# First layer: the values of all heads projected ahead of the attention, with tokens on the partitions, by way of DRAM

## The chip, the cores and the metric

One core of a Trainium2 chip runs the whole program as one launch. The metric is the device time of that launch in microseconds (us), median of several executions. TensorE (PE, with its weight loads PEld), VectorE (DVE), ScalarE (ACT) and GpSimd (POOL) each run their own instructions in order and wait for each other by semaphores; all transfers are issued from SyncE (SP) in one in-order queue.

## What is computed

A model of four layers on 1024 tokens of width 1024. Only the first matters here: RMS norm, one projection into queries, keys and values for three attention groups (dilations 1, 4 and 16) of 16 heads with 64 columns, softmax attention in each, a mix of the three by their log-sum-exps, a gate, and an output projection.

```python
def dilated_attention_mixer(h, w_in, w_out, rel_bias):
    B, S, _ = h.shape
    proj = h @ w_in
    n_qkv = 3 * N_GROUPS_A * ATTN_WIDTH
    qkv = proj[..., :n_qkv].reshape(B, S, 3, N_GROUPS_A, ATTN_HEADS, HEAD_DIM)
    z = proj[..., n_qkv:]
    outs, lses = [], []
    for g, (window, dilation) in enumerate(DILATED_GROUPS):
        o, l = dilated_group_attention(qkv[:, :, 0, g], qkv[:, :, 1, g], qkv[:, :, 2, g],
                                       rel_bias, window, dilation)
        outs.append(o)
        lses.append(l)
    wts = jax.nn.softmax(jnp.stack(lses), axis=0)
    o = jnp.sum(wts[..., None] * jnp.stack(outs).astype(jnp.float32), axis=0)
    o = o.reshape(B, S, ATTN_WIDTH).astype(h.dtype)
    return (o * jax.nn.silu(z)) @ w_out
```

The second layer is a state-space mixer whose tables (powers and kernels from a_re, a_im, log_dt, b, c) don't depend on the tokens. The third and fourth are scaled and shifted by "modulations", products of one vector with w_mod_2, which don't depend on the tokens either. Both are prepared during the first layer.

## The kernel before, in words

All large products are made in three parts: an operand is split into a high part in a format that TensorE takes at full rate (fp32r) and a rest, and high x high, high x rest and rest x high are summed (`mm3`, line 158; its matmuls are all line 168). A tile of 512 columns over a depth of 1024 is 24 matmuls. ScalarE rounds a weight chunk (`w_split`, line 154: wh), VectorE takes the rest (line 155: wl). `stream` (line 1023) keeps four chunks of 512 KB on their way and one split ahead.

`attn` (line 240) first loads the eight tiles of x, normalizes them (`prenorm`) and turns them into aTh and aTl, the normalized input with features on the partitions, split (`to_aT`, lines 215 to 221). The projections start among that: `stream` is opened after the fourth tile.

Then it goes over 8 head pairs p and, within each, 3 groups g. `project(p, g)` (line 312) makes queries, keys and values, each a column of 128 features by 1024 tokens in two halves (`proj_cm`): 6 halves of 24 matmuls. For g below 2 the queries and keys are split by ScalarE and VectorE out of the accumulator (lines 351 and 353) and GpSimd copies the key's parts (line 357). The values are copied by ScalarE into a tile `v` in the order of the dilation (line 343). `steps` (line 377) makes a list of functions: two `vtr`, each of which transposes four 128x128 pieces of `v` on TensorE (line 385) and copies them to V by VectorE (line 386), then ten functions with scores S (lines 399 to 404), the masked row minimum (VectorE, line 412), exponentials (ScalarE, line 414), transposes of them (line 425) and the product with V (lines 132 and 135).

These functions are put on a background list `self.bg`. Every eighth matmul of a projection is a tick, and `tick` takes as many functions from the list as `pace` has set, so that the steps of one group run among the projections of the next. On the same list come `finish` of a head pair (five functions, lines 460 to 538: the statistics turned and passed through DRAM, the weights of the three groups, the weighing and the sum, mostly on VectorE), `ssm_setup` (line 611: five functions, then for each of eight blocks `ca` on GpSimd, `kmat`, and `wj` on VectorE and TensorE, all of which use the one buffer u_A in turn) and the 24 modulations (`mod_jobs`, line 1124: a load of 512 KB, 16 multiply-adds on VectorE of line 1153's form in two functions, and a sum over partitions by ScalarE, GpSimd and TensorE, lines 1159 to 1164). Setup runs in the first eight groups, four functions each; the modulations after it, two per group at first, then one. The tile framework orders each engine's instructions when the program is built, by its own estimate of what is ready.

Of the kernel before, what the change touches and what calls it, by code (L numbers as in the profile page):

```python
# [11 lines left out]
F32 = mybir.dt.float32  # L12
F32R = mybir.dt.float32r
AF = mybir.ActivationFunctionType
# [61 lines left out]
class Ker:  # L76
# [163 lines left out]
    def attn(self, zs):  # L240

        nc, tc, A = self.nc, self.tc, self.A
        w = A["attn_w_in"][0]
# [8 lines left out]
        with ExitStack() as es:  # L252
            qp = es.enter_context(tc.tile_pool(name="qp", bufs=2, reuse_waits="tile"))
            ap = es.enter_context(tc.tile_pool(name="ap", bufs=2, reuse_waits="tile"))
            with ExitStack() as xs:
                p = xs.enter_context(tc.tile_pool(name="l0in", bufs=1, side="right", reuse_waits="tile"))
                g = self.bcast(p, A["attn_pre_norm"][0], "gpre")
                for i in range(8):
                    x = p.tile([128, 1024], F32, tag="x", name=self.uid("x"), bufs=2)
                    nc.sync.dma_start(x, A["x"][0, i * 128:(i + 1) * 128, :])  # L260
                    self.to_aT(self.prenorm(p, x, g), i)
                    if i == 3:
                        weights = self.stream([(w, c) for c in cols])
                self.attn_tables(p)
            side = es.enter_context(ExitStack())
            sp = side.enter_context(tc.tile_pool(name="su", bufs=1, side="right", reuse_waits="tile"))
            setup = deque(self.ssm_setup(sp))
# [43 lines left out]

            def project(p, g):
                T = {}
# [4 lines left out]
                for what in range(3):  # L318
# [4 lines left out]
                    if what == 2:  # L323
                        T[2] = tile_("v", F32, 1)
                    elif split:
# [9 lines left out]
                    for hf in range(2):  # L335
                        ps = self.proj_cm(h, l, hf * 512, parts=1 if p or g or what else 2)
# [5 lines left out]
                        if what == 2 or not split:  # L342
                            nc.scalar.activation(at(T[what], g, hf), pv, AF.Copy, scale=sc)
                            continue
# [32 lines left out]
            def steps(p, g, T, bt, st, O):  # L377
                V = ap.tile([128, 8, 128], F32, tag="V", name=self.uid("V"), bufs=1)
                vT = T[2]

                def vtr(hf):
                    t = self.pt()
                    for k in range(4):
                        c = (hf * 4 + k) * 128
                        nc.tensor.transpose(t[:, k * 128:(k + 1) * 128], vT[:, c:c + 128], self.ident)
                    nc.vector.tensor_copy(V[:, hf * 4:hf * 4 + 4, :], t.rearrange("p (k n) -> p k n", n=128))

# [60 lines left out]
                out = [lambda: vtr(0), lambda: vtr(1)]  # L448
# [91 lines left out]
            fin, mods = None, None  # L540
            for p in range(8):
# [3 lines left out]
                for g in range(3):  # L545
                    self.pace(18)
# [3 lines left out]
                    if g == 0 and fin:  # L550
                        todo.insert(1, fin[0])
                        todo.insert(5, fin[1])
                        todo.insert(9, fin[2])
                        todo.insert(12, fin[3])
                        todo.append(fin[4])
                    if setup:
                        for k in range(min(4, len(setup))):
                            todo.insert(2 + 4 * k, setup.popleft())
                        if not setup:
                            todo.append(side.close)  # L560
                    elif mods is None:
# [1492 lines left out]
```

## Time and profile before

| | us |
|---|---|
| median of 3 runs | 3239.62 |
| lowest and highest | 3238.14, 3244.05 |
| the profiled execution, own time | 3247.39 |
| its span | 3245.4 |
| first layer up to its gates | about 1150 of the span |

The profile is of one execution on one core. It lists what each engine was busy with, in which order, and what ended its idle time. Instructions of one engine overlap, TensorE's above all: the time that a matmul is listed with is longer than the distance to the next.

### The profile page before, as it was taken

The page shows a single profiled execution, that of the slowest core. Times are in us where ns is not written, and L with a number is a line of the kernel's source. Part 1 is how long each engine was busy: PE and PEld are TensorE (multiplying, and loading weights), DVE is VectorE, ACT ScalarE, POOL GpSimd, SP SyncE. Part 2 cuts the span into 40 slices and gives each one's busy share as a digit, 9 for nine tenths or more (in the row PEclk, how much of TensorE's full clock was granted, in tenths as well). Part 3 has the DMA queues.
Part 4 walks back from the last instruction along what each step waited for, and adds up shares of the span by engine and source line. Part 5 has one row for each costly group of instructions (what it writes and reads, how often), then busy time and mean ns, then how long its engine had stood idle before and what let it go on. Part 6 is the DMA issues. An engine that isn't in the chain of part 4 may idle for free. (4 is left out here: it accounts for less than half of the span.)

```text
span 3245.4 us, 48179 instructions
## 1 busy us (share of the span) xinstructions
PE 3119.8 (96%) x18340; PEld 2576.7 (79%) x18340; DVE 1925.1 (59%) x4147; ACT 1210.5 (37%) x2496; POOL 578.3 (18%) x769
## 2 busy tenths in 40 slices
PE   7999999999999999999999999999999999999998
PEld 6888787877778788787878888778887888778777
DVE  5565668777775748565644634454557854445555
ACT  4544444444444554322432122244352212134351
POOL 1244402121111201111003023200002212210001
PEclk9999999999999999999999999999999999999999
DMA  4222233332322225565342211142224321133232
GB/s 137 59 86 91 83 92 100 97 95 87 99 88 72 74 90 179 182 176 156 130 136 91 66 46 50 48 119 73 73 80 161 101 69 56 46 101 88 72 113 97
DMA packets 325210, 312.86 MB, mean 96 GB/s; under 512 B 27801, under 2 KB 277364, under 8 KB 324980
## 3 DMA queue, kind: packets, MB, share of 16 engines
q1 hardware_dynamic: 324980, 309.80, 31.4%
q8 instruction: 144, 2.36, 0.3%
q14 instruction: 86, 0.70, 0.1%
HBM read 249.64 MB, written 60.09 MB: 95 GB/s over the span
## 5 line engine op out<-in xcount | busy, mean ns | idle before, releaser
L168 PE MATMUL mm<-aTh,wh 128*128 128x512 f32 (+1 forms) x2704 | 1076.6, 398 | 26.6 <-DVE qk L353 9.8
L168 PE MATMUL mm<-aTl,wh 128*128 128x512 f32 (+1 forms) x2704 | 1075.0, 398 | 0.7 <-DVE aTl L221 0.3
L168 PE MATMUL mm<-aTh,wl 128*128 128x512 f32 (+1 forms) x2704 | 1070.1, 396 | 0.8 <-DVE wl L155 0.8
L168 PEld LDWEIGHTS mm<-aTh,wh 128*128 128x128 f32 x2704 | 513.4, 190 | 136.4 <-issue 8.2
L168 PEld LDWEIGHTS mm<-aTh,wl 128*128 128x128 f32 x2704 | 513.2, 190 | 102.6 <-issue 3.7
L168 PEld LDWEIGHTS mm<-aTl,wh 128*128 128x128 f32 x2704 | 513.8, 190 | 100.6 <-issue 5.4
L155 DVE TENSOR_TENSOR wl<-wr,wh 128x1024 fp32r<-128x1024 f32 x176 | 220.9, 1256 | 183.8 <-ACT wh L154 181.9
L154 ACT ACTIVATE wh<-wr 128x1024 fp32r<-128x1024 f32 x176 | 186.0, 1057 | 362.9 <-PE mm L168 297.7
L414 ACT ACTIVATE sb<-sb,st 128x128 f32<-128x128 f32 (+1 forms) x384 | 170.4, 445 | 278.3 <-DVE st L412 277.0
L168 PE MATMUL mm<-wo,aTh 128*128 128x512 f32 x768 | 242.4, 397 | 7.9 <-DVE ys L1955 4.6
L412 DVE CUSTOM_DVE_ANT_0 sb<-S,bt 128x128 f32<-128x128 f32 (+1 forms) x384 | 126.4, 343 | 116.9 <-PE T L425 92.3
L1153 DVE SCALAR_TENSOR_TENSOR ma<-mw,cact,ma 128x256 f32<-128x256 f32 x336 | 174.0, 530 | 15.6 <-DMA mw<-in_w_mod 10.0
L168 PEld LDWEIGHTS mm<-wo,aTh 128*128 128x128 f32 x768 | 144.5, 190 | 38.7 <-DVE ys L1955 5.0
L168 PE MATMUL mm<-wo,aTl 128*128 128x512 f32 x384 | 151.8, 395 | 0.9 <-DVE aTl L1900 0.9
L1717 ACT ACTIVATE nsb<-nsb,nmn 128x640 f32<-128x640 f32 (+1 forms) x108 | 85.6, 793 | 117.9 <-DVE nmn L1714 105.5
L1160 POOL TENSOR_TENSOR ms<-ma,ms 128x256 fp32r<-128x256 f32 x48 | 40.2, 837 | 413.9 <-ACT ms L1159 301.8
L357 POOL CAST qk<-kz 64x512 fp32r<-64x512 f32 x64 | 65.8, 1028 | 252.7 <-ACT kz L351 250.6
L425 PE MATMUL T<-ident,sb 128*128 128x128 f32 x560 | 99.3, 279 | 11.9 <-ACT PT L428 8.1
L168 PE MATMUL mm<-cTh,wl 128*128 128x256 f32 x352 | 101.9, 289 | 0.6 <-DVE wl L155 0.6
L168 PE MATMUL mm<-cTl,wh 128*128 128x256 f32 x352 | 102.0, 290 | 0.0
L168 PE MATMUL mm<-cTh,wh 128*128 128x256 f32 x352 | 101.4, 288 | 0.0
L1710 DVE CUSTOM_DVE_ANT_0 nsb<-S,zero 128x256 f32<-128x256 f32 x108 | 45.0, 421 | 84.2 <-PE T L1748 30.3
(443 smaller groups left out, 5221.1 us busy)
## 6 DMA issues: line engine op xcount, KB each, us to landing
wr<-in_attn_w_in SPq DMA_DIRECT2D x80, 512.0 KB
wr<-in_w_in SPq DMA_DIRECT2D x64, 512.0 KB
mw<-in_w_mod SPq DMA_DIRECT2D x48, 512.0 KB
tab<-in_c_rpb SPq DMA_DIRECT2D x72, 192.0 KB
Wb<-wgd SPq DMA_DIRECT2D x96, 128.0 KB
x<-x SPq DMA_DIRECT2D x24, 512.0 KB
x<-in_x SPq DMA_DIRECT2D x16, 512.0 KB
wr<-in_ssm_w_in SPq DMA_DIRECT2D x16, 512.0 KB
```

The source lines that it names most:

```text
L154: nc.scalar.activation(h, raw, AF.Copy)
L155: nc.vector.tensor_tensor(l, raw, h.bitcast(F32), op=ALU.subtract)
L168: nc.tensor.matmul(out, s_, m_, start=first and i == 0, stop=last and i == len(todo) - 1)
L357: nc.gpsimd.tensor_copy(at(t[o], g, hf), at(h_[r], g, hf))
L412: nc.vector.tensor_tensor_reduce(out=sb[:, :N], in0=sp[:, a * 256:a * 256 + N], in1=b, scale=1.0, scalar=3e38, op0=ALU.add, op1=ALU.min, a ...
L414: nc.scalar.activation(sb[:, :N], sb[:, :N], AF.Exp, bias=mc, scale=-1.0, accum_out=st[:, 1, g, a, n:n + 1])
L425: nc.tensor.transpose(t[:, c:c + 128], Ps[a][:, b * 128:b * 128 + 128], self.ident)
L1153: V.scalar_tensor_tensor(a, L[h][:, k], c, a, op0=ALU.mult, op1=ALU.add)
L1160: nc.gpsimd.tensor_tensor(l_, L["a", i], h.bitcast(F32), op=ALU.subtract)
L1710: V.tensor_tensor_reduce(out=sb[:, 0:256], in0=C, in1=zero.to_broadcast([128, 256]), scale=-0.125, scalar=3e38, op0=ALU.add, op1=ALU.min, ...
L1717: ACT.activation(sb[:, :n], sb[:, :n], AF.Exp, bias=mc, scale=-1.0, accum_out=den)
```

## The change

- The values of all heads and groups are projected first: six blocks of 512 value columns, each in eight tiles of 128 tokens by 512 columns (`v_tile`). The activations aTh and aTl are the standing operand, the weights the moving one, so that tokens come out on the partitions. ScalarE copies a tile to SBUF, and it is stored in DRAM (vd, six arrays of 1024x512).
- The first block runs among the loading and normalizing of x: its tile i − 1 after x tile i.
- During the other 40 tiles, `ssm_setup` whole and nine modulations run on the background list, interleaved evenly and paced over 116 ticks.
- In the groups, `project` makes queries and keys alone (4 halves), `values` loads V from vd in the order of the dilation (one transfer for dilation 1, two each for 4 and 16) into one of two buffers, and the two `vtr` are gone. The pace is 12 ticks in place of 18.
- The 15 modulations that are left are spread evenly over the 24 groups; `finish` stands at every third place of the list.

The core of the diff:

```diff
-                cols += [t * 3072 + g * 1024 + p * 128 for t in range(3)]
+                cols += [t * 3072 + g * 1024 + p * 128 for t in range(2)]
...
+                def v_split(u):
+                    if u < 24:
+                        hl = [vp.tile([128, 1024], F32R, tag=x, name=self.uid(x), bufs=6) for x in ("vh", "vl")]
+                        if u % 4 == 0:
+                            hl = None
+                        wv[u] = [t.rearrange("p (k n) -> p k n", n=512) for t in self.w_split(raws.popleft(), hl)]
+                        v_raw(u + 4)
+
+                def v_tile(j, i):
+
+                    ps = self.mm()
+                    tt = slice(i * 128, i * 128 + 128)
+                    self.mm3(ps, [((self.aTh[:, k, tt], self.aTl[:, k, tt]),
+                                   tuple(t[:, k % 2] for t in wv[j * 4 + k // 2])) for k in range(8)])
+                    o = vp.tile([128, 512], F32, tag="vo", name=self.uid("vo"), bufs=3)
+                    nc.scalar.activation(o, ps, AF.Copy)
+                    nc.sync.dma_start(vd[j][tt, :], o)
...
+                            self.to_aT(self.prenorm(p, x, g), i)
+                        if i:
+                            v_tile(0, i - 1)
+                    self.attn_tables(p)
...
+                first = [mods.popleft() for _ in range(9)]
+                jobs = [f for a, b in zip(first + [()], [()] + first) for f in (*a[:1], *b[1:])]
+                self.bg.extend(setup[:5])
+                n, m = len(setup) - 5, len(jobs)
+                order = sorted([(i / n, f) for i, f in enumerate(setup[5:])] +
+                               [(i / m, f) for i, f in enumerate(jobs)], key=lambda t: t[0])
+                self.bg.extend(f for _, f in order)
...
+                self.pace(116)
+                for j in range(1, 6):
+                    for i in range(8):
+                        v_tile(j, i)
+                        if i % 2:
+                            v_split(j * 4 + 4 + i // 2)
+                weights = self.stream([(w, c) for c in cols])
+                self.drain()
...
+            def values(p, g):
+
+                V = ap.tile([128, 8, 128], F32, tag="V", name=self.uid("V"), bufs=2)
...
             def project(p, g):
-                T = {}
+                T = {"V": values(p, g)}
...
-                for what in range(3):
+                for what in range(2):
...
-                out = [lambda: vtr(0), lambda: vtr(1)]
+                out = []
...
-                    self.pace(18)
+                    self.pace(12)
...
+                        for k, f in enumerate(fin):
+                            todo.insert(1 + 3 * k, f)
+                    if len(mods) * 24 > left * (23 - p * 3 - g):
+                        for k, f in enumerate(mods.popleft()):
+                            todo.insert(2 + 3 * k, f)
```

How the built program's order moves. First, TensorE at its beginning. T is an accumulator tile for transposes, xn a normalized tile of x, mm a projection's accumulator. Before:

```order
L215 MATMUL T_123<-ident,xn_115 128x128 x4
L215 MATMUL T_130<-ident,xn_115 128x128 x4
L215 MATMUL T_147<-ident,xn_139 128x128 x4
L215 MATMUL T_154<-ident,xn_139 128x128 x4
L168 MATMUL mm_412<-aTh,wh_217 128x256
L168 MATMUL mm_412<-aTl,wh_217 128x256
L168 MATMUL mm_412<-aTh,wl_218 128x256
```

And now:

```order
L215 MATMUL T_126<-ident,xn_118 128x128 x4
L215 MATMUL T_133<-ident,xn_118 128x128 x4
L168 MATMUL mm_198<-wh_152,aTh 128x512
L168 MATMUL mm_198<-wl_153,aTh 128x512
L215 MATMUL T_184<-ident,xn_176 128x128 x4
L168 MATMUL mm_198<-wh_152,aTl 128x512
```

The first projection needs one tile of x and not two, in matmuls of 512 columns in place of 256.

Second, TensorE within a group before, where the values' transposes stand among the projections; v is the values' tile:

```order
L168 MATMUL mm_656<-aTl,wh_588 128x512
L168 MATMUL mm_656<-aTh,wl_589 128x512
L168 MATMUL mm_656<-aTh,wh_588 128x512
L385 MATMUL T_673<-ident,v_594 128x128 x4
L168 MATMUL mm_656<-aTl,wh_588 128x512
```

And TensorE among the V tiles now, at the first of setup's eight blocks; u_A and u_bd are setup's operands, vh and vl a split weight piece:

```order
L168 MATMUL mm_1246<-vl_1183,aTh 128x512
L132 MATMUL T_1017<-u_A_922,u_bd 32x128
L135 MATMUL T_1017<-u_A_922,u_bd 32x128 x3
L168 MATMUL mm_1246<-vh_1182,aTl 128x512
L168 MATMUL mm_1301<-wh_798,aTh 128x512
```

No row with v as an operand is left in the program; setup's small products now stand between V tiles, at fixed places in the order.

Third, VectorE at the block after that. ma is a modulation's running sum, mw its weights, u_br, u_pr and u_pi setup's tables:

```order
L860 TENSOR_TENSOR u_C_1263<-T_1270,u_dd_1268 128x16
L834 TENSOR_TENSOR u_A_1356<-u_br,u_pr 128x128 x4
L834 TENSOR_TENSOR u_A_1356<-u_br,u_pi 128x128 x4
L1205 SCALAR_TENSOR_TENSOR ma_1510<-mw_1237,cact,ma_1510 128x256
L855 TENSOR_SCALAR u_dd_1551<-u_eye,u_d 128x16
L836 TENSOR_TENSOR u_A_1356<-u_A_1356,u_B_1357 128x512
L1205 SCALAR_TENSOR_TENSOR ma_1510<-mw_1239,cact,ma_1510 128x256
L835 TENSOR_TENSOR u_B_1357<-u_bi,u_pr 128x128 x4
L1205 SCALAR_TENSOR_TENSOR ma_1510<-mw_1239,cact,ma_1510 128x256
L836 TENSOR_TENSOR u_A_1356<-u_A_1356,u_B_1357 128x512
```

Before, a block's products stood among the masked minima and copies of the attention:

```order
L808 TENSOR_TENSOR u_C_1481<-T_1488,u_dd_1486 128x16
L782 TENSOR_TENSOR u_A_1578<-u_br,u_pr 128x128 x4
L782 TENSOR_TENSOR u_A_1578<-u_br,u_pi 128x128 x4
L412 ISA sb_1513,st_400<-S_1508,bt_391 128x128
L412 ISA st_400 128x1
```

The multiply-adds of the modulations have taken the place of the attention's instructions between a block's products.

## Rows read from the trace of the kernel before

**Rows 1.** The page, part 1: engine, busy us, share of the span, instructions.

```profile
PE 3119.8 (96%) x18340; PEld 2576.7 (79%) x18340; DVE 1925.1 (59%) x4147; ACT 1210.5 (37%) x2496; POOL 578.3 (18%) x769
```

**Rows 2.** Timeline of TensorE, attention layer: start us, us, engine, line, operation.

```profile
443.06 0.40 PE L168 MATMUL mm<-aTh,wl 128*128 128x512 f32 x1
443.30 0.60 PE L425 MATMUL T<-ident,sb 128*128 128x128 f32 x4
443.65 0.48 PE L168 MATMUL mm<-aTh,wh 128*128 128x512 f32 x1
443.96 0.39 PE L168 MATMUL mm<-aTl,wh 128*128 128x512 f32 x1
444.19 0.40 PE L168 MATMUL mm<-aTh,wl 128*128 128x512 f32 x1
```

**Rows 3.** Stretches: TensorE, weight loads, VectorE, ScalarE, GpSimd busy us; clock; DMA share, GB/s.

```profile
0.00:62.00 62.00, 43.54 (x243) 35.47 (x244) 33.59 (x52) 29.82 (x54) 15.82 (x34) 1.00 0.52 149
62.00:1160.00 1098.00, 1055.36 (x6220) 870.41 (x6218) 753.13 (x2008) 520.45 (x1278) 252.88 (x328) 0.99 0.29 86
62.00:114.00 52.00, 49.55 (x265) 41.24 (x264) 42.20 (x142) 26.62 (x53) 14.62 (x23) 1.00 0.24 67
```

**Rows 4.** Three groups (head pair, dilation) as stretches: the columns of rows 3.

```profile
158.00:203.00 45.00, 45.00 (x275) 37.16 (x274) 22.76 (x76) 20.83 (x58) 21.23 (x40) 1.00 0.26 81
526.00:580.00 54.00, 48.76 (x286) 39.49 (x286) 39.92 (x92) 23.97 (x60) 11.01 (x9) 0.97 0.32 101
812.00:866.00 54.00, 48.67 (x284) 39.54 (x283) 42.19 (x97) 23.89 (x58) 11.20 (x10) 0.97 0.37 109
```

**Rows 5.** Groups of TensorE instructions, 0 to 1215 us: transposes of V.

```profile
L385 PE MATMUL T<-ident,v 128*128 128x128 f32 x192 | 30.2, 278 | 0.8 <-ACT PT L428 0.8
```

**Rows 6.** Groups of VectorE instructions, 62 to 1160 us: busy us, mean ns, idle before.

```profile
L1153 DVE SCALAR_TENSOR_TENSOR ma<-mw,cact,ma 128x256 f32<-128x256 f32 x336 | 174.0, 530 | 15.6 <-DMA mw<-in_w_mod 10.0
L155 DVE TENSOR_TENSOR wl<-wr,wh 128x1024 fp32r<-128x1024 f32 x70 | 89.6, 1280 | 34.5 <-ACT wh L154 32.9 <-PE mm L168 1.3
L386 DVE COPY V<-T 128x512 f32<-128x512 f32 x46 | 30.3, 681 | 1.4 <-PE T L385 1.1
L784 DVE TENSOR_TENSOR u_A<-u_A,u_B 128x512 f32<-128x512 f32 x16 | 10.9, 679 | 0.1
L782 DVE TENSOR_TENSOR u_A<-u_br,u_pr 128x128 f32<-128x128 f32 x32 | 10.2, 373 | 1.0 <-DMA cad<-u_A 1.0
L782 DVE TENSOR_TENSOR u_A<-u_br,u_pi 128x128 f32<-128x128 f32 x32 | 8.5, 311 | 0.0
```

**Rows 7.** Line 168, 0 to 62 us: ns min/median/max, first and last start, forms.

```profile
L168 PE MATMUL mm<-aTh,wh x54: 278/386/580, 16.8 to 61.6; 128*128 128x256 f32 x32, 128*128 128x512 f32 x22
L168 PE MATMUL mm<-aTl,wh x54: 278/388/582, 17.6 to 61.8; 128*128 128x256 f32 x32, 128*128 128x512 f32 x22
L168 PE MATMUL mm<-aTh,wl x53: 278/285/416, 17.9 to 61.3; 128*128 128x256 f32 x32, 128*128 128x512 f32 x21
```

**Rows 8.** Products of setup and of a modulation, by tile and line: ns min/median/max.

```profile
L766 POOL TENSOR_TENSOR u_A<-u_cb,u_pr x32: 435/442/1429, 103.0 to 381.0; 128x144 f32<-128x144 f32 x32
L768 POOL TENSOR_TENSOR u_A<-u_A,u_B x16: 1398/1424/1438, 113.2 to 391.0; 128x576 f32<-128x576 f32 x16
...
L1153 DVE SCALAR_TENSOR_TENSOR ma<-mw,cact,ma x336: 448/484/1730, 423.5 to 1103.1; 128x256 f32<-128x256 f32 x168
```

**Rows 9.** Timeline of GpSimd: a block's products, first and last.

```profile
163.95 1.65 POOL L766 TENSOR_TENSOR u_A<-u_cb,u_pr 128x144 f32<-128x144 f32 x4 [8.04 <-PE T L790]
...
170.40 1.42 POOL L768 TENSOR_TENSOR u_A<-u_A,u_B 128x576 f32<-128x576 f32 x1
```

**Rows 10.** Timeline of VectorE: a block's products, first and last.

```profile
148.54 1.00 DVE L782 TENSOR_TENSOR u_A<-u_br,u_pr 128x128 f32<-128x128 f32 x4
...
153.44 0.69 DVE L784 TENSOR_TENSOR u_A<-u_A,u_B 128x512 f32<-128x512 f32 x1
```

**Rows 11.** Tile u_A: the first TensorE instructions of the eight blocks, first and last start.

```profile
L132 PE MATMUL T<-u_A,u_bd x16: 272/284/297, 147.5 to 390.0; 128*32 128x128 f32 x16
```

More of the change, by code (lines that the diff above doesn't have):

```diff
@@ L253, in attn @@
             qp = es.enter_context(tc.tile_pool(name="qp", bufs=2, reuse_waits="tile"))
             ap = es.enter_context(tc.tile_pool(name="ap", bufs=2, reuse_waits="tile"))
[L255 to L264, printed above, removed]
@@ L310, in shaped_q, with src @@
                 return ps.rearrange("p (l n d) -> p l n d", n=8, d=2)
+            def values(p, g):
+                V = ap.tile([128, 8, 128], F32, tag="V", name=self.uid("V"), bufs=2)
+                t = vd[g * 2 + p // 4]
+                o = t.offset + p % 4 * 128
+                def src(off, ap_):
+                    return bass.AP(tensor=t.tensor, offset=o + off * 512, ap=[[x * 512, n] for x, n in ap_] + [[1, 128]])
+                if g == 0:
+                    nc.sync.dma_start(V, src(0, [[1, 128], [128, 8]]))
+                elif g == 1:
+                    Vv = V.rearrange("p (r b) n -> p b r n", b=2)
+                    for b in range(2):
+                        nc.sync.dma_start(Vv[:, b], src(b * 512, [[4, 128], [1, 4]]))
+                else:
+                    for d in range(2):
+                        nc.sync.dma_start(V[d * 64:d * 64 + 64], src(d, [[16, 64], [2, 8]]))
+                return V
             def project(p, g):
-                T = {}
+                T = {"V": values(p, g)}
                 split = g < 2
@@ L335, in project @@
                     for hf in range(2):
-                        ps = self.proj_cm(h, l, hf * 512, parts=1 if p or g or what else 2)
+                        ps = self.proj_cm(h, l, hf * 512)
                         pv = (shaped if what else shaped_q)(ps, g)
@@ L341, in project @@
                             continue
-                        if what == 2 or not split:
+                        if not split:
                             nc.scalar.activation(at(T[what], g, hf), pv, AF.Copy, scale=sc)
@@ L377, in steps @@
             def steps(p, g, T, bt, st, O):
[L378 to L386, printed above, removed]
+                V = T["V"]
                 live = {}
@@ L538, in finish @@
                 return f0, f1, f2, f3, f34
[L540 removed]
+            fin, left = None, len(mods)
             for p in range(8):
@@ L550, in attn @@
                     if g == 0 and fin:
[L551 to L561, printed above, removed]
-                        mods = deque(self.mod_jobs(side.enter_context(
-                            tc.tile_pool(name="mo", bufs=1, side="right", reuse_waits="tile"))))
-                    for _ in range(2 if mods and len(mods) > 23 - (p * 3 + g) else 1):
-                        if mods:
-                            for k, f in enumerate(mods.popleft()):
-                                todo.insert(2 + 3 * k, f)
+                        for k, f in enumerate(fin):
[3 more added lines that the diff above has]
+                            todo.insert(2 + 3 * k, f)
                     self.bg.extend(todo)
@@ L570, in attn @@
             self.bg.extend(fin)
+            while mods:
+                self.bg.extend(mods.popleft())
+                self.drain()
             side.close()
```

33 lines of the change are left out of this document (27 added, 6 removed).

## The prediction

> **What bounds the kernel now.** I read the engine shares first. TensorE is busy 96% of the span and the next engine 59% [rows 1], so a change pays through TensorE or not at all. Busy is not yet work, though: a 512-column matmul is listed with 0.39 us, but the next one starts 0.23 us later [rows 2]. I therefore price TensorE work by the distance between starts, and use "busy" only to find idle time. Second, the stretches: in the first 62 us TensorE is idle for 62 − 43.5 = 18.5 us, in the following 1098 us for 43 us (4%), while VectorE is busy 69% of that time and ScalarE 47% [rows 3]. So the attention layer is a TensorE stream with small holes and a poor start. Last, the holes by group: an undisturbed group of head pair and dilation takes 44 to 45 us with no idle time; one in which a pair is finished, or two modulations run, takes 54 us, of which 5 are idle, at a clock of 0.97, with VectorE busy for 40 and 42 us [rows 4]. Where TensorE waits in this layer, VectorE is the reason.
>
> **The change part by part.**
> (a) Projections. 24 columns x 2 halves x 24 matmuls = 1152 wide matmuls become 6 x 8 tiles x 24 = 1152. The weights now move and the activations stand; both operands are 128x128 against 128x512 as before. Nothing for TensorE.
>
> (b) Transposes of V go: 192 on TensorE [rows 5], in 48 insertions of four. The list shows 278 ns for one. What four in a row cost is the distance around them: from the start of the matmul at 443.06 to that of the second matmul behind the transposes at 443.96 is 0.90 us; the two wide matmuls among it are 2 x 0.23, so four transposes with their two changes of operand cost 0.44 us [rows 2] (the transposes there are another tile's, of the same form). 48 x 0.44 = **21 us off TensorE**. The Trainium skill (TensorE: Matmul & The Clock Gate, Part 4: PE-mode transpose) gives about 275 ns for a transpose in a kernel; the mean in the list agrees with it, but by it the sum would be 192 x 0.275 = 53 us, 32 more than by the distance between starts, which decides. With them go 48 VectorE copies of 0.68 us [rows 6], 33 us in all; I give no time for it by itself, since it counts only where VectorE is late. ScalarE's copy out of the accumulator stays, as one copy per tile.
>
> (c) The start. Until 62 us TensorE now issues 161 projection matmuls from 16.8 us on, 96 of them half as wide [rows 7], worth 65 + 48 = 113 wide ones, 26 us. After the change the first V column block can run one tile per tile of x, and its first matmul needs the same things (first x, first weights). From 16.8 to 62 there are 45.2 us, less 64 transposes of x in fours (16 x 0.44 = 7) and about 3 us of small things: 35 us. The gain is 9 us at most. It needs all four weight pieces of 512 KB split by the first tile and x tiles 2 to 7 behind them in SP's queue, so some is lost; the bounds are 0 and −9, I take **−6**, nearer the upper one, because V tiles last 24 x 0.23 = 5.5 us each and the input chain is shorter than that by its VectorE and ScalarE parts.
>
> (d) Setup and nine modulations beside the other 40 V tiles, which last 40 x 5.5 = 221 us, some 240 with the TensorE part of setup and modulations. VectorE there: block products 10.2 + 8.5 for one half, about as much for the other, and 10.9, together 48; setup's head, at most the 42 us that VectorE was busy from 62 to 114 [rows 3], of which I take half, 21, since attention steps ran there too; nine of 24 modulations 65 plus some 15 for their first and last instructions; 20 weight splits x 1.28 = 26 [rows 6]. That is 175 of 240 us, 73%, a little above now. GpSimd, whose key copies now stand behind all of setup: 128 narrow products at 0.44 and 16 at 1.42 [rows 8], 79 us. Each of the eight blocks is a chain through one buffer (u_A): GpSimd 163.95 to 171.8, 7.9 us [rows 9]; VectorE 148.5 to 154.1, 5.6 us [rows 10]; with matmuls and transposes between them some 16 us. A block's share of the phase is 4 tiles and its own work, about 24 us. So the chain fits with 8 us to spare. Unknown is how often TensorE, in order, stands in front of a late one: bounds 0 and 8 x 2 us; I take **+5**, nearer the lower, since with the chain spread over 35 us per block now TensorE hardly waits for it.
>
> (e) The groups get shorter: 4 projected halves (22 us) instead of 6 (33), the same ten attention steps. What hid VectorE's lateness was projection, and a third of it leaves. Against that, VectorE loses in each group two copies (1.4 us) and a split (1.3), and the modulations thin out, from 24 in 15 groups to 15 in 24. One modulation is 174.0 / 24 = 7.3 us plus its first and last instructions, some 8.3. In the worst groups, with two of them, VectorE is busy 41 of 54 us, 76% [rows 4]; after, with 15 in 24 groups (0.6 in each, 1.4 fewer), that is 41 − 2.7 − 1.4 x 8.3 = 27 of 34 us, 79%. The same share, so I leave the 43 us of idle time as it is, less **4** for the doubled modulations. Bounds: −20 (half of the idle time goes with them) and +28 (rival 2).
>
> (f) DMA. 48 stores of V and 40 loads (one for dilation 1, two each for 4 and 16) join SP's queue, and setup's and nine modulations' issues move ahead of the attention. The weight loads behind them are four columns ahead, 4 x 11 us of use; V is loaded a whole group before its use into one of two buffers. A store waits for ScalarE's copy, and behind it stand weight pieces that are needed a whole column block (44 us) later. I cost all this at nothing; its cover is these leads, and if they went, each late load would stop TensorE for its own time.
>
> Sum: −21 − 6 + 5 − 4 = **−26 us**, the profiled execution's 3247.4 becoming 3221. That execution was 7.8 us above the median of the runs, 3239.6, from which the forecast is **3214 us**.
>
> **The rivals.**
> 1. *The holes go too.* If lighter VectorE work in the groups removes half of the idle time and the clock drops that follow it, (e) is −20 or more and the time 3180 to 3198. For it: idle time is thickest where two modulations run [rows 4]. Against: where none runs, a finish still comes in every third group.
> 2. *The attention takes it back.* Where a pair is finished while the next group is projected, VectorE is left with 41 − 2.7 − 8.3 = 30 us of work, one modulation among it, against 33 us of TensorE. If VectorE sets the pace of the seven intervals with a finish, each 4 us longer, clock drops included, 28 us come back: 3242, no change; half of it gives 3228. For it: these are the intervals that wait today. Against: the 54 us of today hold more VectorE work still.
> 3. *Slower: setup sets the pace of the V phase.* The pieces of TensorE's setup work stand in a fixed order between V tiles. Today a block comes every (390.0 − 147.5) / 7 = 35 us [rows 11]; the new order wants one every 24. It decides if the chain of (d) takes more than 24 us: at 35, eight blocks would hold TensorE for 8 x 11 = 88 us, and the time is 3300; already at 28 it is 3246. For it: GpSimd's product of 0.44 us has taken up to 1.43 [rows 8], and a modulation's of 0.48 up to 1.73 us [rows 8]; both engines are now full at once. Against: the 35 us are where the program put the blocks, and GpSimd then also copied keys and weighed outputs. The Trainium skill (GPSIMD Engine Reference, 1. Specifications) says that GpSimd shares its SBUF interface with VectorE and contends with VectorE instructions that have two SBUF inputs, which is what a modulation's and a block's products are; the maxima of these rows agree with it, and it speaks against the place that the change chooses.
>
> That the change might not do what it says is excluded by the order: no transpose of V is left in it.
>
> **How the numbers follow.** Forecast, −14 to −40: 0.62. Rival 1: 0.14. Rival 2: 0.15. Rival 3 or any other loss: 0.09. Differences within 0.2%, 6.5 us, can't be told from none. The first two are faster, of rival 2 a quarter: 0.80; the rest of it is the same: 0.11; slower 0.09. The range leaves out rival 3 and the far end of rival 1: 3182 to 3240.
>
> **What would show it.** Right: no transposes of V; TensorE nearly closed from 17 us to the end of the V phase near 320 us, eight blocks some 24 us apart; then 24 groups of about 33 us; idle time of the attention layer near 40 us. Wrong: TensorE's waits for u_A or for a modulation's sums amount to tens of us in the V phase (rival 3), or groups with a finish that take 40 us and more (rival 2). A forecast by TensorE's work fails if the groups stop being bound by it.

## The result and the profile after

The changed kernel takes 3215.7 us (median of 4 runs, 3213.1 to 3217.7) beside 3241.8 for the kernel before on the same chip: a ratio of 0.9914, 95% interval 0.9897 to 0.9931, or 26 us less (28 by the ratio). Forecast were 3214 us and a sum of −26. The total is right; the experiments below show that terms behind it are not.

The profiled execution of the changed kernel took 3217.5 us (span 3215.5), that of the kernel before 3247.4 (span 3245.4). Part 1 of its page, to be read against [rows 1]:

```profile
PE 3103.7 (97%) x18100; PEld 2549.1 (79%) x18100; DVE 1898.8 (59%) x4099; ACT 1194.1 (37%) x2494; POOL 592.2 (18%) x769
```

TensorE has 240 instructions fewer: the 192 transposes of V, and 48 because 96 half-wide matmuls are now 48 wide ones. VectorE has the 48 copies fewer.

**Where the first layer ends.** A row that both programs have is ScalarE's first work for the second layer's gates (columns: ns min/median/max, first and last start). Before:

```profile
L977 ACT ACTIVATE sz<-mm x16: 577/598/602, 1377.5 to 1588.6; 128x512 f32<-128x512 f32 x16
```

After:

```profile
L1029 ACT ACTIVATE sz<-mm x16: 577/600/602, 1351.5 to 1562.6; 128x512 f32<-128x512 f32 x16
```

The two are 26.0 us apart at either end. All of the gain is made in the first layer; what the spans differ by beyond it (29.9 in all) comes in layers that the change does not touch; single executions of one kernel differ by as much.

**The stretches**, with the columns of [rows 3]: start, V phase, groups, end of the layer.

```profile
0.00:62.00 62.00, 50.78 (x235) 41.22 (x236) 30.05 (x36) 30.43 (x48) 7.73 (x24) 1.00 0.59 205
62.00:312.00 250.00, 248.59 (x1218) 194.06 (x1217) 173.29 (x460) 62.54 (x100) 119.46 (x194) 1.00 0.54 169
312.00:1120.00 808.00, 777.30 (x4704) 637.89 (x4703) 553.78 (x1507) 438.88 (x1172) 151.66 (x143) 0.99 0.31 90
1120.00:1190.00 70.00, 68.46 (x387) 56.34 (x386) 31.36 (x83) 34.58 (x79) 5.37 (x3) 1.00 0.33 96
```

TensorE is idle for 11.2 us in the start (before 18.5), for 1.4 in the V phase and for 30.7 in the groups. After 62 us that makes 33.6 us, where before it was 43 [rows 3]. The V phase is the quiet part: VectorE is busy for 173 of 250 us there, 69%, and yet TensorE is never late.

**The start**, line 168 until 62 us, to be read against [rows 7]. The rows for vl with aTh and vh with aTl have the same count as the first, those for wl with aTh and wh with aTl the same as the second:

```profile
L168 PE MATMUL mm<-vh,aTh x42: 387/389/628, 17.4 to 60.7; 128*128 128x512 f32 x42
...
L168 PE MATMUL mm<-wh,aTh x15: 387/397/795, 12.1 to 61.4; 128*128 128x512 f32 x15
```

That is 3 x 42 + 3 x 15 = 171 wide matmuls, against 113 before, and the first stands at 12.1 us and not at 16.8. By 62 us the kernel before had also done 18 small matmuls which the changed one does later: 12 scores and six of the attention's tables, among them

```profile
L235 PE MATMUL T<-oh,ra 33*16 33x384 f32 x6 | 2.4, 488 | 0.0
L403 PE MATMUL S<-qk,qk 128*128 128x256 f32 x4 | 1.1, 306 | 0.0
```

By the starts around them these 18 take about 3.7 us.

**The V phase**: GpSimd's products of a block and the blocks' first matmuls, against [rows 8] and [rows 11].

```profile
L818 POOL TENSOR_TENSOR u_A<-u_cb,u_pr x32: 440/448/1469, 114.0 to 282.0; 128x144 f32<-128x144 f32 x32
...
L132 PE MATMUL T<-u_A,u_bd x16: 272/285/297, 124.2 to 290.5; 128*32 128x128 f32 x16
```

The blocks come every (290.5 − 124.2) / 7 = 23.8 us, which is the 24 us that the V tiles allow; before, 35 us. GpSimd's product takes 448 ns in the median, beside a VectorE full of modulations, where it took 442; the median hides a part of them that takes three times as long (rival 3 below).

**The groups**, as stretches between the first copies of the queries of two groups that follow each other (the columns of the stretches above). Five of them; the second, fourth and fifth have a finish in them and are the three longest of the seven that have one:

```profile
340.20:372.20 32.00, 32.00 (x195) 26.91 (x195) 23.31 (x55) 21.12 (x48) 8.20 (x8) 1.00 0.17 50
433.90:473.60 39.70, 36.42 (x217) 29.68 (x217) 35.84 (x80) 21.63 (x50) 14.75 (x12) 0.96 0.38 110
504.30:535.60 31.30, 31.30 (x197) 26.04 (x196) 21.56 (x71) 16.63 (x57) 3.91 (x5) 1.00 0.30 87
535.60:577.10 41.50, 36.88 (x218) 29.94 (x217) 37.30 (x84) 22.41 (x54) 17.19 (x12) 0.95 0.36 105
741.30:781.20 39.90, 36.06 (x217) 28.70 (x214) 34.48 (x79) 20.19 (x44) 10.05 (x9) 1.00 0.33 95
```

The two without a finish take 31 to 32 us with no idle time; the three with one take 40 to 41, with VectorE busy for 34 to 37 of them (86 to 90%), TensorE idle for 3 to 5, and twice a lower clock. Not all are like these. The sums and means over all seven with a finish (31.0 to 41.5 us long, from 433.9 us on), and over the 14 without one from 372.2 to 1056.4 us (29.4 to 40.1 us long):

```profile
sum 262.50, PE 244.57 PEld 198.40 DVE 227.14 ACT 145.51 POOL 73.15; mean PE 34.94 PEld 28.34 DVE 32.45 ACT 20.79 POOL 10.45
sum 452.70, PE 440.39 PEld 362.93 DVE 267.07 ACT 241.84 POOL 54.35; mean PE 31.46 PEld 25.92 DVE 19.08 ACT 17.27 POOL 3.88
```

That is 37.5 us on average with a finish and 32.3 without. The same seven and fourteen intervals of the kernel before sum to

```profile
sum 340.80, PE 321.46 PEld 261.75 DVE 275.74 ACT 171.59 POOL 104.80; mean PE 45.92 PEld 37.39 DVE 39.39 ACT 24.51 POOL 14.97
sum 650.10, PE 631.61 PEld 523.82 DVE 413.32 ACT 295.89 POOL 126.86; mean PE 45.12 PEld 37.42 DVE 29.52 ACT 21.14 POOL 9.06
```

or 48.7 and 46.4 us on average: the intervals with a finish have become 11 us shorter, the others 14.

**TensorE's waits until 1190 us** (us in total, times, longest), the largest, and two further ones:

```profile
PE T L215 <- DVE xn L205: 9.9, 1, 9.9
PE S L464 <- DVE st L473: 9.4, 9, 3.2
PE S L464 <- DVE qk L423: 6.5, 3, 3.9
PE T L486 <- DVE mr L1216: 4.5, 4, 1.4
...
PE T L135 <- POOL u_A L820: 1.0, 2, 0.7
...
PE T L1214 <- POOL ms L1212: 0.8, 1, 0.8
```

The scores' accumulators (S, three of them, released by VectorE's masked minima of line 473) are, behind the start, what is waited for most. For V from DRAM there is no wait.

### The profile page after: what moved, and what is told of

The parts are those of the page before. It is cut to its first block, busy times and chain, and to the rows that moved or that the text cites. A ratio compares the mean times of both kernels' runs of the same rounds, so it can differ in the third digit from the quotient of the medians.

```text
span 3215.5 us, 47884 instructions
## 1 busy us (share of the span) xinstructions
PE 3103.7 (97%) x18100; PEld 2549.1 (79%) x18100; DVE 1898.8 (59%) x4099; ACT 1194.1 (37%) x2494; POOL 592.2 (18%) x769
## 5 line engine op out<-in xcount | busy, mean ns | idle before, releaser
L168 PE MATMUL mm<-aTh,wh 128*128 128x512 f32 x2304 | 920.7, 400 | 18.2 <-DVE nk L1480 2.8
L168 PE MATMUL mm<-aTl,wh 128*128 128x512 f32 x2304 | 917.4, 398 | 0.4 <-DVE aTl L221 0.2
L168 PE MATMUL mm<-aTh,wl 128*128 128x512 f32 x2304 | 916.1, 398 | 0.7 <-DVE wl L155 0.7
L168 PEld LDWEIGHTS mm<-aTh,wh 128*128 128x128 f32 x2304 | 437.5, 190 | 110.2 <-issue 5.4
L168 PEld LDWEIGHTS mm<-aTh,wl 128*128 128x128 f32 x2304 | 436.8, 190 | 88.5 <-issue 3.4
L168 PEld LDWEIGHTS mm<-aTl,wh 128*128 128x128 f32 x2304 | 437.7, 190 | 85.3 <-issue 2.9
L155 DVE TENSOR_TENSOR wl<-wr,wh 128x1024 fp32r<-128x1024 f32 x158 | 196.8, 1245 | 191.4 <-ACT wh L154 190.8
L473 DVE CUSTOM_DVE_ANT_0 sb<-S,bt 128x128 f32<-128x128 f32 (+1 forms) x384 | 125.2, 345 | 46.3 <-PE T L486 30.2
L168 PE MATMUL mm<-vh,aTl 128*128 128x512 f32 x288 | 114.5, 398 | 0.0
L168 PE MATMUL mm<-vh,aTh 128*128 128x512 f32 x288 | 113.8, 395 | 0.0
L168 PE MATMUL mm<-vl,aTh 128*128 128x512 f32 x288 | 113.6, 394 | 0.0
```

The costliest lines, as they stand in the source:

```text
L155: nc.vector.tensor_tensor(l, raw, h.bitcast(F32), op=ALU.subtract)
L168: nc.tensor.matmul(out, s_, m_, start=first and i == 0, stop=last and i == len(todo) - 1)
L473: nc.vector.tensor_tensor_reduce(out=sb[:, :N], in0=sp[:, a * 256:a * 256 + N], in1=b, scale=1.0, scalar=3e38, op0=ALU.add, op1=ALU.min, a ...
```

## The experiments

The theory was that of the prediction: the transposes are worth the distance that they take among TensorE's starts, and VectorE's work counts only where it is late. All ratios are to the kernel before on the same chip. The changed kernel, run a second time among the experiments, gave 0.9913 (0.9899 to 0.9927); differences from it are worked out from the ratios with 3243 us, and one of these has an uncertainty of about 6 us (two intervals of 0.14% each, 0.2% together); most of them compare runs on different chips, each by way of the kernel before. "End of layer" is the last start of the row on sz above, in the run's own profile.

| run | ratio to before (95%) | us against before | us against changed | end of layer |
|---|---|---|---|---|
| before | 1 | 0 | | 1588.6 |
| changed, first time | 0.9914 (0.9897 to 0.9931) | −28 | | 1562.6 |
| changed, second time | 0.9913 (0.9899 to 0.9927) | −28 | 0 | 1558.6 |
| before without copies of V | 0.9945 (0.9932 to 0.9959) | −18 | | 1581.4 |
| before without transposes and copies | 0.9914 (0.9901 to 0.9928) | −28 | | 1569.0 |
| changed + transposes | 0.9959 (0.9946 to 0.9971) | | +15 | 1581.0 |
| changed + transposes + one-column copies | 1.0006 (0.9995 to 1.0017) | | +30 | 1587.5 |
| changed + transposes + copies | 1.0045 (1.0032 to 1.0057) | | +43 | 1609.1 |
| changed + VectorE work alone | 0.9920 (0.9903 to 0.9936) | | +2 | 1563.2 |
| changed, no modulation beside V | 0.9938 (0.9925 to 0.9951) | | +8 | 1568.3 |
| changed, 15 modulations beside V | 0.9912 (0.9893 to 0.9931) | | 0 | 1560.9 |
| changed, nothing beside V | 1.0119 (1.0103 to 1.0135) | +39 | +67 | 1629.3 |
| changed, last part of finish later | 0.9881 (0.9864 to 0.9899) | −39 | −10 | 1553.5 |
| changed, product copied by ScalarE | 0.9898 (0.9881 to 0.9916) | | −5 | 1552.1 |

### The transposes and their copies, taken out of the kernel before

```diff
-                V = ap.tile([128, 8, 128], F32, tag="V", name=self.uid("V"), bufs=1)
...
+                V = vT.rearrange("p (k n) -> p k n", n=128)
...
-                    nc.vector.tensor_copy(V[:, hf * 4:hf * 4 + 4, :], t.rearrange("p (k n) -> p k n", n=128))
```

The tile `v` gets two buffers in place of one. In the second kernel `vtr` goes altogether. Expected of the first:

> The kernel before with the transposes of V kept, but not VectorE's 48 copies of them (the product takes the values untransposed). Theory: 0 to 4 us less than before, 3236 to 3240. Rival A: the same as the theory here. Rival B: 10 to 25 us less, 3215 to 3230.

And of the second:

> The kernel before without the two functions that turn V: no transposes of V on TensorE, no copies of them on VectorE (the product takes the values untransposed, so this part of the computation is changed). Theory (distance between starts: 0.44 us for an insertion of four): 21 us less than before, 3219. Rival A (listed duration, 275 ns each): 53 us less, 3187. Rival B (TensorE's holes are VectorE's lateness, so the 48 copies of 0.68 us count as well): 30 to 45 us less, 3195 to 3210.

Measured: 18 us less without the copies, 28 without both, so 10 for the transposes. By the ends of the layer the two steps are 7 and 12 us. Rival A, the listed 275 ns each, is out. The 18 lie in rival B's range, the 28 between the theory's 21 and the 30 with which rival B begins. The theory has the transposes too dear and the copies too cheap: most of the gain hangs on 48 copies to which the prediction gave no time.

Both profiles lose some 5 us in the start, which the edit does not touch: the granted clock is 0.89 there where it is 1.00 before [rows 3], and by 62 us 140 and 138 projection matmuls are done in place of 161, the missing ones 512 columns wide. Of the second kernel:

```profile
0.00:62.00 62.00, 42.38 (x214) 33.81 (x215) 28.95 (x39) 25.20 (x42) 14.03 (x32) 0.89 0.47 135
```

Behind 62 us the two steps are therefore some 12 and 13 us in these profiles. Whether the other executions have this start too, no record shows.

TensorE's waits for the scores' accumulators, which VectorE's masked minima release, were in the kernel before (62 to 1250 us)

```profile
PE S L403 <- DVE st L412: 5.0, 6, 2.2
PE S L399 <- DVE st L412: 3.0, 2, 1.6
```

and without the copies

```profile
PE S L402 <- DVE st L411: 0.2, 1, 0.2
```

### Put back into the changed kernel

```diff
+                def vtr(hf):
+                    t = self.pt()
+                    for k in range(4):
+                        nc.tensor.transpose(t[:, k * 128:(k + 1) * 128], V[:, hf * 4 + k], self.ident)
+                    vj = ap.tile([128, 512], F32, tag="vj", name=self.uid("vj"), bufs=1)
+                    nc.vector.tensor_copy(vj, t)
...
-                out = []
+                out = [lambda: vtr(0), lambda: vtr(1)]
```

Expected of the transposes alone (without the last two lines of `vtr`), and with the copies:

> The changed kernel with the 192 transposes alone put back, without the copies. Theory: 21 us more than the changed kernel, 3237, and within 4 us of the version with the copies. Rival A: 53 us more, 3269. Rival B: 15 to 21 us more, and 10 to 20 us less than the version with the copies.

> The changed kernel with the two functions put back at the head of each group's list, on V as it was loaded: 192 transposes on TensorE and 48 copies on VectorE into a tile that nobody reads. Theory: 21 us more than the changed kernel, 3237. Rival A: 53 us more, 3269. Rival B (the shorter groups are bound by VectorE, now 28 of 35 us): 30 to 45 us more, 3246 to 3261.

Measured: +15 (by the ends of the layer 18 to 22) and +43. The transposes alone fit the theory's 21 within the uncertainty; the copies add 28 more, where the theory had at most 4, so rival B comes nearest, in the upper half of its range. What TensorE waits for from 312 to 1190 us with the copies:

```profile
PE S L471 <- DVE st L480: 15.5, 12, 3.2
PE S L467 <- DVE st L480: 11.7, 9, 1.6
PE mm L168 <- DVE qk L423: 7.3, 10, 1.4
```

The first two are waits of a score for an accumulator that a masked minimum has not yet released: 27 us against 9.4 in the changed kernel, which had none of them in groups of dilation 16 (here line 467). But VectorE, over the same layer (62 to 1190 us), is far from full and waits itself, for transposes of exponentials (30.2 us in the changed kernel):

```profile
DVE sb L480 <- PE T L493: 104.3, 46, 4.8
```

So the two engines wait for each other in turn. Two readings are left: VectorE's time, or the accumulators that hang between the engines.

### VectorE's time alone

```diff
+                def vcp(hf):
+                    vj = ap.tile([128, 4, 128], F32, tag="vj", name=self.uid("vj"), bufs=1)
+                    v = V[:, hf * 4:hf * 4 + 4]
+                    nc.vector.tensor_tensor(vj, v, v, op=ALU.add)
...
-                out = []
+                out = [lambda: vcp(0), lambda: vcp(1)]
```

> The changed kernel with 48 VectorE additions of 128x512 (0.68 us each, 33 us in all) put where the copies of the transposes were put before, with nothing on TensorE: they read the loaded V and write a tile that nobody reads. If the copies cost their 25 to 28 us because VectorE, in order, comes later to the masked minima that release TensorE's score accumulators: 20 to 28 us more than the changed kernel, and TensorE's waits for those minima grow as they did with the copies. If they cost it because a copy holds one of the two accumulators for transposes: 0 to 8 us more. If only VectorE's share of the time counts (69%, with this 73%): within 5 us.

Measured: +2. The additions took what they should (one row of its VectorE groups, 312 to 1120 us), and VectorE even stood in front of them until V had landed:

```profile
L453 DVE TENSOR_TENSOR vj<-V 128x512 f32<-128x512 f32 x46 | 33.6, 731 | 46.2 <-DMA V<-vd 44.7 <-DMA cm<-statd 1.0
```

34 us of work and 46 of standing cost nothing that can be measured. The framework issues them as soon as V is expected, which is not where it put the copies; but a price per microsecond of VectorE time, wherever it stands, is excluded by this run.

### The accumulator held, without the time

Against the version with the copies:

```diff
-                    nc.vector.tensor_copy(vj, t)
+                    nc.vector.tensor_copy(vj[:, 0:1], t[:, 511:512])
```

> The changed kernel with the transposes of V put back and a copy behind each insertion that reads one column in place of 512: VectorE loses almost no time by it, but each accumulator for transposes is held, as with the full copies, until VectorE has come to its copy in order. If holding the accumulator (one of two) is what the copies cost: as with the full copies, 38 to 46 us more than the changed kernel. If it takes both, the time of the copies and their place between TensorE and the minima: as with the transposes alone, 14 to 22 us more. In between: both count.

Measured: +30, between the transposes alone (+15) and the full copies (+43), each step about 2.5 times as large as its uncertainty of some 5.5 us. By the rule set ahead, both count: the place of the copy and its length. By the ends of the layer the steps are 6.5 and 21.6; the profiled execution of this version took 3237.6 us, the median of its twelve 3247.3.

What the place does is seen in TensorE's waits, here with the one-column copies (62 to 1250 us):

```profile
PE S L467 <- DVE st L480: 11.8, 9, 1.6
PE S L471 <- DVE st L480: 8.7, 9, 3.2
PE T L453 <- DVE vj L455: 1.9, 2, 1.1
PE T L493 <- DVE vj L455: 0.7, 2, 0.4
```

The first two are again scores behind a masked minimum, the last two are transposes behind an accumulator that a copy (vj) holds. In all versions (us; idle is TensorE's, from 62 us to the first start of the row on sz):

| | against changed | idle | scores behind a minimum | transposes behind a copy of V |
|---|---|---|---|---|
| changed | 0 | 41.0 | 9.4 | |
| + transposes | +15 | 46.4 | 13.8 | |
| + transposes + one-column copies | +30 | 53.3 | 20.5 | 2.6 |
| + transposes + copies | +43 | 63.9 | 27.2 | 2.0 |
| + VectorE work alone | +2 | 43.5 | 12.5 | |

So the accumulator that a copy holds is hardly waited for itself. What grows are the waits for the minima, which stand behind the copies in VectorE's order: VectorE stands in front of the one-column copies for 9.0 us until TensorE has made the transposes, and the minima with it. Their growth, 7 us with each kind of copy, is about half of what the step costs; the rest is not seen in a row. VectorE's additions above stood 46 us in front of V and cost nothing, so standing alone is not it; that it is the place ahead of the minima is the reading that is left, and no run shows it by itself. The programs also differ in where the framework puts the instructions around; that part was not separated.

### What stands beside the V tiles

Expected with none of the modulations there, and with 15 in place of nine (`first` has 0 or 15 of them; without any, the rule that spreads them is changed too, so that two go on the first group's list and one on each further but the last):

```diff
-                first = [mods.popleft() for _ in range(9)]
+                first = [mods.popleft() for _ in range(15)]
```

> The changed kernel with no modulation beside the V tiles; all 24 run in the groups. New theory (from the copies put back: 33 us of VectorE work in the groups cost about 25 us, since a late masked minimum holds TensorE's scores): nine modulations are 75 us of VectorE work, so 35 to 57 us more than the changed kernel. Old theory (the groups keep their idle time as long as VectorE's share stays below 80%; it goes from 69 to 78%): 8 to 20 us more. Rival (it does not matter where they run): within 4 us.

> The changed kernel with 15 modulations beside the V tiles and 9 in the groups. VectorE in the V phase goes from 173 to 223 of 250 us, in the groups from 554 to 504 of 808. New theory: 20 to 38 us less in the groups, if the V phase holds. Old theory: 4 to 10 us less. Rival (setup and modulations set the pace of the V phase, as in the prediction's third rival): 10 to 40 us more, with TensorE waiting for u_A or for a modulation's sums.

And with setup too in the groups, by the code of the kernel before:

```diff
-                self.bg.extend(setup[:5])
...
-                self.bg.extend(f for _, f in order)
...
+                    if setup:
+                        for k in range(min(4, len(setup))):
+                            todo.insert(2 + 4 * k, setup.popleft())
```

> The values projected first with nothing beside them; setup in the first eight groups and the 24 modulations in the other 16, as in the kernel before. VectorE's work in the groups goes from 554 to 701 us. New theory: 60 to 110 us more than the changed kernel. Old theory: 25 to 45 us more. Rival (all that counts is that the transposes and copies are gone): within 6 us of the changed kernel.

Measured: +8, 0 and +67. The new theory, a price for each microsecond of VectorE, falls a second time with the first two; in the first, +8 is the lower end of the old theory's range, and in the second 0 can't be told from its −4. The third, +67, lies in the new theory's range and outside the old one's. Stretches of the run without modulations beside V, its V phase and its groups:

```profile
62.00:302.00 240.00, 239.32 (x1175) 191.38 (x1175) 97.42 (x309) 55.34 (x81) 95.34 (x179) 1.00 0.43 140
302.00:1130.00 828.00, 789.30 (x4767) 655.11 (x4766) 620.80 (x1657) 443.99 (x1186) 155.47 (x158) 0.98 0.34 99
```

Of the run with 15:

```profile
62.00:320.00 258.00, 250.81 (x1215) 196.25 (x1214) 198.31 (x502) 63.58 (x105) 131.79 (x195) 0.99 0.54 170
320.00:1130.00 810.00, 779.27 (x4744) 644.55 (x4743) 534.22 (x1475) 442.85 (x1177) 148.97 (x144) 0.97 0.31 89
```

Of the run with nothing beside V, the groups with setup and those with the modulations:

```profile
285.00:560.00 275.00, 263.81 (x1636) 218.91 (x1636) 171.09 (x508) 142.23 (x352) 106.98 (x174) 0.99 0.30 88
560.00:1190.00 630.00, 562.71 (x3293) 460.13 (x3292) 501.00 (x1327) 311.70 (x847) 142.44 (x141) 0.93 0.37 109
```

VectorE's share in the groups is 66% (15), 69% (nine), 75% (none) and, in the last of these rows, 80%; TensorE's idle share is 3.8%, 3.8%, 4.7% and 10.7%, with a clock of 0.97, 0.99, 0.98 and 0.93. Up to 75% the place of the modulations matters little (8 us); in the last row the groups fall behind. There TensorE waits for the masked minima once more, from 285 to 1190 us:

```profile
PE S L455 <- DVE st L464: 32.9, 19, 4.1
PE S L451 <- DVE st L464: 11.1, 12, 2.1
```

The share alone does not explain it. Over all groups of this run (285 to 1190 us) it is 672 of 905 us, 74%, no more than without modulations beside V; but 24 modulations stand in 15 groups where there they stand in 23. How much is due to setup and how much to this packing was not separated. And the V phase begins to wait with 15: 7.2 us idle against 1.4. Nine is no sharp optimum, but setup had to go somewhere else, and beside V there was room.

### Two places where the groups wait

```diff
-                def f34():
-                    weigh(0)
-                    f4()
-                return f0, f1, f2, f3, f34
+                return f0, f1, f2, f3, lambda: weigh(0), f4
...
-                        for k, f in enumerate(fin):
+                        for k, f in enumerate(fin[:5]):
...
+                    if g == 1 and fin:
+                        todo.insert(2, fin[5])
```

> The changed kernel with the last function of a finish (two VectorE additions of 2 us over the three groups' outputs) taken from behind GpSimd's weighing and put a few functions into the next group's list. In the changed kernel VectorE stands in front of these additions for 20.8 us in seven groups until GpSimd is done. If that standing is what makes the seven intervals with a finish last 37 us on average, against 31 for the others: 8 to 18 us less than the changed kernel. If VectorE's total work in those intervals makes them long (the additions move, but stay on VectorE): 0 to 5 us less. If they are long by TensorE's own work or by the DMA round trip: within 3 us.

Measured: −10, in the first case's range near its small end, but with an uncertainty of some 7 us not clear of the second; by the ends of the layer −5 to −9. The cause that was expected is not shown, though: VectorE still stands in front of the addition, 22.4 us,

```profile
L591 DVE TENSOR_TENSOR Os<-Os,Os 128x1024 f32<-128x1024 f32 x7 | 14.0, 2003 | 22.4 <-POOL Os L579 22.4
```

where it was 20.8 (same row of the changed kernel, 312 to 1120 us). What the move changed instead stays open. At 0.9881 of the kernel before it is the fastest version that ran.

```diff
-                    nc.vector.tensor_copy(ov, o.rearrange("p (n i) -> p n i", i=128)[:, :, ::-1])
+                    nc.scalar.activation(ov, o.rearrange("p (n i) -> p n i", i=128)[:, :, ::-1], AF.Copy)
```

> The changed kernel with the 48 copies of the product with V (0.69 us each) moved from VectorE to ScalarE. VectorE loses 33 us of work and 30 us of standing in order until the product is there. If VectorE's place in the order sets TensorE's pace in the groups, as for the copies of the transposes: 10 to 25 us less than the changed kernel. If ScalarE's order is as tight (it then stands in front of the product, with the exponentials behind it): 0 to 25 us more.

Measured: −5, less than the uncertainty (by the ends of the layer −6.5 to −10.5). Neither case is decided.

## Why the prediction was right, and where its terms were not

**(a) Projections, 0.** The wide tiles of the V phase run with 1.4 us of idle time in 250; nothing speaks against the zero.

**(b) V's transposes, −21.** Mis-sized and misplaced. In the kernel before, both parts together are worth 28 us: 10 for the transposes and 18 for the copies, where the step said "I give no time for it by itself, since it counts only where VectorE is late". A copy is more than VectorE's time: it stands in VectorE's order between TensorE's transposes and the masked minima, and TensorE's scores wait for these (8.0 us in the kernel before, 0.2 without the copies). The distance between starts (21) stands at the upper end of what the transposes alone were worth (10 in the one kernel, 15 in the other, by single profiles 12 to 22). The sum by the Trainium skill's duration (TensorE: Matmul & The Clock Gate, Part 4: PE-mode transpose), 53 us, is excluded by both kernels; the list's own 278 ns [rows 5] agreed with that duration all the same. A duration of a pipelined instruction is no price.

**(c) The start, −6, bounds 0 and −9.** Mis-sized, but less than the matmuls alone say: 171 − 113 = 58 wide ones more by 62 us, at 0.23 us, are 13 us; the 18 small ones that then still have to be done take 3.7 of them back. That leaves about 10, at the edge of the bounds. The step let the first matmul stay at 16.8 us. It needs one tile of x now and not two, as the order ahead of the prediction shows, and came at 12.1.

**(d) Beside the V tiles, +5.** Right in kind, a little too dear: 1.4 us of idle time, blocks 23.8 us apart where 24 were forecast, VectorE at 69% where 73% were forecast. What the term did not say is what this place was worth: with setup and modulations left to the groups the kernel is 67 us slower.

**(e) The groups, −4, bounds −20 and +28.** The idle time that the profile shows fell by 9 us (43 to 33.6). But the kernel before without V's transposes and copies is as fast as the changed one (0.9914 both), though the latter has about 10 us less at the start; so V phase and groups must give about as much back. The single profiles agree: by 62 us the changed kernel is 81 wide matmuls ahead, 19 us less some 3 for small ones, and at the end of the layer (1569.0 and 1562.6) only 6. This is worked out from differences and not seen in a row. It lies inside the bounds, on the other side from the −4. Where it goes stays open: TensorE's idle time from 62 us to the first start of the row on sz is the same, 41.6 us in that kernel and 41.0 in the changed one.

**(f) DMA, 0.** No wait of TensorE for V, for its stores or for weights behind them is in the list.

So −28 − 10 and some 10 back make −28 by the ratios; the prediction had −21 − 6 + 5 − 4 = −26. The copies, left out, and the start, too small, were offset by what the V phase and the groups took back. The forecast came out by more luck than its working shows.

**Rival 1** (the holes go too): 9 us of 43, no more. **Rival 2** (the attention takes it back): its mechanism is there, and nearly in its size. The seven intervals with a finish last 37.5 us on average where 33 were forecast for all, with VectorE busy for 32.5 of them, and its sign, "groups with a finish that take 40 us and more", came in one of them and nearly in two (41.5, 39.9, 39.7). Two things kept the forecast right all the same: the others need 32.3, and the copies' 18 us, which no term had, went the other way. Before, these seven were only 2.3 us longer than the others, now 5.2. **Rival 3** (slower): not beside V, where the waits for u_A are 1.4 us in all; but a kernel that ends on the other side exists, 39 us slower than before, and it is the one that projects V first and leaves setup and modulations where they were. The fear behind it has a ground that the product's median, 448 ns and 442 before, does not show. Where a subtraction of a weight split, which reads two tiles from SBUF, runs beside them, GpSimd's products take about as long as it does. Here are four in a row, which take 0.44 us each when alone:

```profile
160.66 3.69 POOL L818 TENSOR_TENSOR u_A<-u_cb,u_pr 128x144 f32<-128x144 f32 x4 [2.01 <-PE T L842]
```

and VectorE at the same time:

```profile
160.58 1.23 DVE L155 TENSOR_TENSOR vl<-wr,vh 128x1024 fp32r<-128x1024 f32 x1 [0.60 <-ACT vh L154]
162.41 1.23 DVE L155 TENSOR_TENSOR vl<-wr,vh 128x1024 fp32r<-128x1024 f32 x1 [0.60 <-ACT vh L154]
```

The first and the third of the four take 1.45 and 1.47 us, the other two 0.44. These rows agree with the contention of GpSimd with VectorE instructions of two SBUF inputs that the Trainium skill describes (GPSIMD Engine Reference, 1. Specifications). The chain of a block had room for it: what the rival feared happens, but it hardly reaches TensorE.

## What to carry to other kernels

Price a copy out of an accumulator by what stands behind it in its engine's order and who waits for that, and not by the copying engine's load: here 34 us of plain VectorE work cost 2, and 48 copies of the same length behind transposes 28. When a projection is moved away from work that it hid, something of that work must move with it; the same V phase is worth −28 us or +39, by what stands beside it. And check a right total by its terms: take each out of the old kernel and put it back into the new one.

## What was not expected of the hardware

In the stretch where VectorE is busy 80% of the time, TensorE's idle share goes to 10.7% and the granted clock to 0.93, where at 75% they are 4.7% and 0.98. It is one run, its modulations stand closer together, and over all of its groups VectorE's share is 74%: a mean share of an engine says little about when another one that waits for it falls behind.

A GpSimd product of 128x144 that takes 0.44 us takes 1.45 beside a VectorE subtraction of 128x1024 from two tiles; a median over all products hides it.
